# Loading the first shift vector ahead of the first weights of a decoder trunk

## The chip, the cores and the metric

The kernel runs on one core of a Trainium2 chip: TensorE for matmuls, VectorE, ScalarE and GpSimd for elementwise work, and SyncE (SP), which issues the transfers from HBM. They run beside each other and are ordered by semaphores alone; each does its own instructions in program order. The metric is the device time of one execution in microseconds. Before the change it is 1204.11 us, the median of 3 runs (1202.5 to 1204.75).

## The reference

Two layers, each with a half-step SwiGLU FFN, a token-mixing sub-layer and a second half-step FFN, all modulated by vectors that are computed from c; batch 1, 256 positions, 1024 channels, FFN width 2816.

```python
def modulate(x, g, shift, scale):
    return rmsnorm(x, g) * (1 + scale[:, None, :]) + shift[:, None, :]

c_act = jax.nn.silu(c)
for l in range(DEPTH):
    mod = c_act @ w_ada[l] + b_ada[l]
    sh1, sc1, gt1, sh2, sc2, gt2, sh3, sc3, gt3 = jnp.split(mod, N_MOD, axis=-1)
    h = modulate(x, ln_ffn1_g[l], sh1, sc1)
    x = x + 0.5 * gt1[:, None, :] * swiglu(h, ffn1_w_gate[l], ffn1_w_up[l], ffn1_w_down[l])
    ...
```

Each modulation vector is the product of c_act (1024) with a 1024x1024 part of w_ada, 4 MB of HBM. The change concerns the first two of the program: sc1 and sh1 of layer 0.

## The kernel before

All weights stream through four buffers of 1 MB (`raw`), in granules of one megabyte, in a fixed list (`seq`, filled by `adaunit` and `plan_ffn`). SP issues the transfer of a granule when the one four places ahead of it in the list has been used up. A weight granule holds two units of 128x1024. Each unit is split: ScalarE casts it to a high part (`hi`), and VectorE, or GpSimd for the units that `cfg["lo_first"]` names at the start, subtracts to get the low part (`lo`). There are six buffers for pairs of hi and lo. An FFN block of 128 columns then is 24 matmuls of 128x128 by 128x256: hi weights by hi input, hi by lo, lo by hi, eight each.

A modulation vector comes in four granules. VectorE multiplies each half granule with a column of c_act and adds it to a running sum of 128x1024 (`Lb` or `adaacc`, eight operations in `ada_step`); TensorE turns the sum, and VectorE reduces it to a column per block of 128 channels (`extract`, `complete`).

The list begins with the scale vector sc1 (`adaunit(0, 1, i)`), then come the granules gate 0, up 0 and gate 1 of the first FFN, then the shift vector sh1, then up 1 and so on. FFN blocks run in pairs q: two gate and two up units per q, and the two down units of the pair before.

The shift vector is late, so the first FFN begins without it. `G` holds x scaled by sc1 in high and low parts, not yet divided by the norm of each position (`S6a`, `Q`, `S3a`, `V`, `v`). `first()` runs six raw units on it with `low_last` (gate 0 and 1, up 0 and 1, gate 2 and 3). When the sum of sh1 is there, it multiplies the two-column shift with the same six units' weights (96 small products, `sh_b`) for their biases, and makes the true input H (`modulate`, high part on ScalarE, low part on VectorE; the product `PT` of scaled x and rstd on ScalarE and GpSimd). The raw outputs are multiplied by rstd afterwards (`normed_out`) and get the bias in `first_act`. `columns(0, 1)` transposes constants of the layer (`rowsA`, `rowsB`) into the one PSUM bank `x`, one after the other: the second transpose needs VectorE's copy of the first (`colA`). `keep_warm` issues three products that nobody reads.

The order of instructions on each engine is the order in which this program emits them. `pump` and `done` emit the next conversions of weights whenever a buffer of the six is free by a built-in model of the clock (`Clock`). All instructions are recorded in one helper line, L171; the tiles' names tell them apart.

In later phases sh and sc are known early: the shift then rides along as two more columns of the raw input (258 in place of 256), and four units run block by block in `first_units`.

## Time and profile before

| | |
|---|---|
| median of 3 runs | 1204.11 us |
| profiled execution | 1202.57 us, of which the span shown is 1200.8 us |
| TensorE busy | 1130.7 us (94% of the span) |
| VectorE busy | 874.4 us (73%) |
| ScalarE busy | 612.6 us (51%) |
| GpSimd busy | 169.3 us (14%) |
| mean granted TensorE clock | 0.976 of full speed |

The share of busy time of an engine says little by itself: what counts is which engine the others wait for in a stretch. The profile gives the chain of waits, followed back from the last instruction, and the timeline of each engine with the idle time ahead of an instruction and who ended it. The granted clock is 1.00 at 2.4 GHz and 0.50 at 1.2 GHz.

### The profile page before, as it was taken

The numbers are of one execution on the slowest core, as the hardware profiler recorded it, in microseconds if no ns is written. First come the engines' busy times: TensorE is split into PE (matmuls) and PEld (weight loads), VectorE is DVE, ScalarE is ACT, GpSimd is POOL, SyncE is SP. The second block draws the span as 40 slices with busy tenths as digits, with TensorE's granted clock in tenths as the row PEclk, the third lists the DMA queues.
The fourth block names the chain that finished last, engine by engine and source line by source line (L and its number), as shares of the span: only waits on it lengthen the run. The fifth ranks groups of instructions, "written<-read, shape, count | busy, mean of one in ns | idle before, by whom it ended". The sixth has DMA issues, their size and how long they took to land.

```text
span 1200.8 us, 22053 instructions
## 1 busy us (share of the span) xinstructions
PE 1130.7 (94%) x9085; PEld 1052.0 (88%) x9085; DVE 874.4 (73%) x1314; ACT 612.6 (51%) x1049; POOL 169.3 (14%) x213
## 2 busy tenths in 40 slices
PE   5799999999978789999999999999997899999997
PEld 4799999977767789999999999997876789999996
DVE  5778878757965788877778878774886759866554
ACT  4364443548367464434456544444654667544443
POOL 0610000011761010000000000001067401000001
PEclk9899999999999989999999999999999799999999
DMA  8759888836342558969865987892642334876640
GB/s 320 246 186 319 309 299 309 256 113 192 95 137 91 176 176 285 322 243 326 291 218 170 324 313 266 278 300 74 186 140 73 141 108 140 287 257 211 195 139 36
DMA packets 167661, 256.52 MB, mean 214 GB/s; under 512 B 8272, under 2 KB 134056, under 8 KB 167560
## 3 DMA queue, kind: packets, MB, share of 16 engines
q1 hardware_dynamic: 166536, 252.95, 62.6%
q0 software_dynamic: 1024, 2.16, 0.9%
q8 instruction: 71, 1.16, 0.4%
q14 instruction: 30, 0.25, 0.1%
HBM read 252.86 MB, written 2.23 MB: 212 GB/s over the span
## 4 chain that ended last, share of the span: by engine, by line
PE 71%; DVE 12%; ACT 6%; POOL 6%; issue 3%; DMA 1%; SPq 0%; POOLq 0%; DVEq 0%; ACTq 0%
PE pm L171 45%; PE pa L171 25%; DVE lo L171 3%; DVE adaacc L171 3%; PE px L171 2%; ACT hi L171 1%; POOL W L171 1%; POOL cacc L171 1%; POOL T L171 1%; POOL Lb L171 1%; DVE mod L171 1%; ACT L171 1%; DVE tmp L171 1%; DVE Lb L171 1%; DVE Y L171 1%
## 5 line engine op out<-in xcount | busy, mean ns | idle before, releaser
L171 PE MATMUL pm<-H,hi 128*128 128x256 f32 x2816 | 507.7, 283 | 2.8 <-issue 1.6
L171 DVE TENSOR_TENSOR lo<-raw,hi 128x1024 fp32r<-128x1024 f32 (+1 forms) x300 | 362.1, 1226 | 131.8 <-ACT hi L171 131.3
L171 PEld LDWEIGHTS pm<-H,hi 128*128 128x128 f32 x2816 | 431.9, 189 | 5.9 <-issue 2.2
L171 ACT CAST hi<-raw 128x1024 fp32r<-128x1024 f32 (+1 forms) x306 | 311.3, 1040 | 195.3 <-PE pm L171 80.7
L171 PE MATMUL pm<-H,lo 128*128 128x256 f32 x1408 | 392.4, 280 | 1.2 <-DVE lo L171 1.2
L171 PEld LDWEIGHTS pm<-H,lo 128*128 128x128 f32 x1408 | 264.5, 189 | 1.7 <-DVE lo L171 1.6
L171 PE MATMUL pa<-Y,hi 128*128 128x256 f32 x1312 | 241.3, 286 | 4.5 <-DVE xT L171 4.5
L171 PEld LDWEIGHTS pa<-Y,hi 128*128 128x128 f32 x1312 | 204.1, 192 | 6.7 <-DVE xT L171 5.3
L171 PE MATMUL pa<-Y,lo 128*128 128x256 f32 x656 | 185.8, 283 | 0.0
L171 PEld LDWEIGHTS pa<-Y,lo 128*128 128x128 f32 x656 | 127.3, 194 | 0.0
L171 POOL TENSOR_TENSOR xin_LT<-xin_LT 128x256 f32<-128x256 f32 x35 | 27.1, 775 | 664.8 <-ACT xin_LT L171 662.4
L171 ACT CAST Y<-tmp 128x256 fp32r<-128x256 f32 x88 | 35.8, 406 | 131.5 <-DVE tmp L171 131.5
L171 DVE SCALAR_TENSOR_TENSOR adaacc<-raw,c_act,adaacc 128x1024 f32<-128x1024 f32 x70 | 95.5, 1365 | 1.6
L171 DVE SCALAR_TENSOR_TENSOR Lb<-raw,c_act,Lb 128x1024 f32<-128x1024 f32 x56 | 71.8, 1283 | 4.2 <-DMA raw<-in_w_ada_dram 3.0
L171 POOL TENSOR_TENSOR cacc<-cacc,ctap 128x256 f32<-128x256 f32 x54 | 52.3, 973 | 122.0 <-DVE cacc L171 112.8
L171 DVE TENSOR_TENSOR Y<-tmp,Y 128x256 fp32r<-128x256 f32 x88 | 37.4, 425 | 41.5 <-ACT Y L171 41.5
L171 PE MATMUL pm<-Y,raw 128*128 128x256 f32 x288 | 66.8, 384 | 0.0
L171 PEld LDWEIGHTS pm<-Y,raw 128*128 128x128 f32 x288 | 53.4, 190 | 8.9 <-issue 1.0
L171 PE MATMUL pa<-hi,Y 128*128 128x512 f32 x176 | 54.8, 393 | 0.0
L171 ACT ACTIVATE tmp<-pm 128x256 f32<-128x256 f32 x84 | 31.8, 378 | 43.9 <-PE pm L171 43.7
L171 DVE TENSOR_REDUCE mod<-px 128x4 f32<-128x512 f32 x34 | 23.4, 689 | 34.3 <-PE px L171 34.2
L171 DVE SCALAR_TENSOR_TENSOR cacc<-hc,colB,cacc 128x256 f32<-128x256 f32 x66 | 36.0, 562 | 10.3 <-POOL cacc L171 9.4
(309 smaller groups left out, 1342.9 us busy)
## 6 DMA issues: line engine op xcount, KB each, us to landing
raw<-in_w_ada_dram SPq DMA_DIRECT2D x70, 1024.0 KB
raw<-in_ffn_w_gate_dram SPq DMA_DIRECT2D x44, 1024.0 KB
raw<-in_ffn_w_up_dram SPq DMA_DIRECT2D x44, 1024.0 KB
raw<-in_ffn_w_down_dram SPq DMA_DIRECT2D x44, 1024.0 KB
raw<-in_w_in_dram SPq DMA_DIRECT2D x12, 1024.0 KB
raw<-in_w_in_dram SPq DMA_DIRECT2D x20, 512.0 KB
raw<-in_w_out_dram SPq DMA_DIRECT2D x16, 512.0 KB
raw<-in_w_in_dram SPq DMA_DIRECT2D x4, 768.0 KB
```

The lines of the kernel that those rows point to most:

```text
L171: return getattr(real, op)(*args, **kw)
```

## The change

The granules of sh1 come right behind those of sc1, ahead of all weights. Its sum is shared: of each granule VectorE adds one half into `adaacc`, and TensorE multiplies the other half with a column of c_act into a row of 1x512 in each of two PSUM banks (`ada_rows`); at the end TensorE adds VectorE's sum to the rows with a product with ones, VectorE copies the row out, and eight transposes turn it into columns. The shift is then known ahead of the first unit, so `first()` is the one of the later phases: four units on 258 columns, one unit behind the other (`first_serial`, with `low_last`). The bias products, the raw units of gate 2 and 3 and `keep_warm` are gone. The other modulation vectors in the first FFN start at slot 2 in place of slot 4.

```diff
@@ -309,7 +309,7 @@
-        start = 4 if key == ("f", 0, 1) else 0
+        start = 2 if key == ("f", 0, 1) else 0
@@ -323,9 +323,6 @@
-                if key == ("f", 0, 1) and (q, n) == (1, "g"):
-                    for i in range(4):
-                        adaunit(0, 0, i)
@@ -406,8 +403,9 @@
-    for i in range(4):
-        adaunit(0, 1, i)
+    for v in (1, 0):
+        for i in range(4):
+            adaunit(0, v, i)
@@ -477,9 +475,39 @@
+    def ada_rows(raw, g, i):
+
+        if i == 0:
+            ada_acc[0, 0] = [ps([1, 512], f"a{2 + h}") for h in range(2)] + [sb([128, D], "adaacc")]
+        *rows, acc = ada_acc[0, 0]
+        halves = [slice(512 * h, 512 * h + 512) for h in range(2)]
+        for h in range(2):
+            mm(rows[h], c_act[:, 2 * i + 1:2 * i + 2], raw[:, 1, halves[h]], i == 0, False)
+        c = c_act[:, 2 * i:2 * i + 1]
+        if i == 0:
+            dve.tensor_scalar(acc, raw[:, 0], c, 0.0, op0=OP.mult, op1=OP.add)
+        else:
+            dve.scalar_tensor_tensor(acc, raw[:, 0], c, acc, op0=OP.mult, op1=OP.add)
+        release(g)
+        if i < 3:
+            return
+        row = sb([1, D], "Lb")
+        for h in range(2):
+            mm(rows[h], ones[:, 0:1], acc[:, halves[h]], False)
+            dve.tensor_copy(row[:, halves[h]], rows[h])
+        p = ps([128, KB], "x")
+        for k in range(KB):
+            pe.transpose(p[:, k:k + 1], row[:, 128 * k:128 * k + 128], ident[0:1, 0:1])
+        m = sb([128, KB], "mod0", bufs=2)
+        dve.tensor_copy(m, p)
+        complete(m, 0, 0, slice(0, KB))
+        mods[0, 0] = m
+
...
@@ -773,6 +803,11 @@
+    def first_serial(keys, outs, G, between):
+
+        for i, (key, o) in enumerate(zip(keys, outs)):
+            low_last(o, need(key), G["parts"], between if i == 0 else None)
+
...
@@ -897,93 +928,36 @@
...
-                keep_warm(3)
-                for h in range(2):
-                    extract()
...
-                for h in range(2):
-                    for i, kk in enumerate(keys):
-                        for k in range(4 * h, 4 * h + 4):
-                            for x, w in enumerate(conv[kk]):
-                                mm(p[i // 4][:, i % 4], both[:, k], w[:, k], k == 0 and x == 0 and i % 4 == 0, (k, x) == (KB - 1, 1))
...
+            opening = key == ("f", 0, 1)
+            (first_serial if opening else first_units)(keys, outs, G, lambda: norm.update(h=normed([pump] * 3, opening)))
+            for i in range(2):
+                for j in range(2):
+                    dve.tensor_copy(cols[i][:, j:j + 1], outs[2 * j + i][:, S:S + 1])
+            su = [normed_out(o) for o in outs]
+            acc.extend(ps([128, 2, S], f"a{i}") for i in range(4))
+            for kk in keys:
+                done(kk)
+            if opening:
                 columns(0, 1)
...
+            act.preload_act_table_set("silu_and_others")
+            for i in range(2):
+                first_act(i, su[i], su[2 + i], cols[i][:, 0:1], cols[i][:, 1:2])
+            return norm["h"]
...
@@ -1921,18 +1895,24 @@
-    cfg["lo_first"] = ["gp", "dve", "gp", "dve", "gp", "gp", "dve", "gp", "dve", "gp"]
     columns(0, 0)
-    step_stream()
     gs = need_mod(0, 1)
     G = begin(gs, None)
-    keep_warm(3)
+    rstd(sums)
     for k in range(KB):
         scaled_hi(G, k)
-        scaled_lo(G, k)
-    step_stream()
-    rstd(sums)
-    for _ in range(4):
+    for i in range(4):
+        step_stream()
+        for k in {1: range(4), 2: range(4, KB)}.get(i, ()):
+            scaled_lo(G, k)
+    cfg["lo_first"] = ["gp", "gp"]
+    G["sh"] = mods[0, 0]
+    for _ in range(2):
+        step_stream()
+    G["shift"](G["sh"])
+    for k in range(KB):
+        dve.scalar_tensor_tensor(nscr["t"][:, k], xT[:, k], gs[:, k:k + 1], nscr["r"], op0=OP.mult, op1=OP.mult)
+    for _ in range(2):
         step_stream()
```

Where the instructions stand now. On VectorE, from the last operation on the scale vector (mod_181 in before) to the first transposed constants, in before:

```order
L171 SCALAR_TENSOR_TENSOR mod_181<-mod_181,colA 128x4
L171 SCALAR_TENSOR_TENSOR S3a<-xT,mod_181,S6a 128x256 x3
L171 SCALAR_TENSOR_TENSOR V<-xT,mod_181,S6a 128x256 x3
L171 SCALAR_TENSOR_TENSOR v<-xT,mod_181,Q_199 128x256 x2
L171 TENSOR_TENSOR lo<-raw,hi 128x1024 x2
L171 TENSOR_SCALAR adaacc<-raw,c_act 128x1024
L171 SCALAR_TENSOR_TENSOR adaacc<-raw,c_act,adaacc 128x1024 x7
L171 COPY colA<-px 128x23
L171 COPY colB<-px 128x98
```

The same place now, from the same operation (mod_174 is the scale vector) to the shift vector, mod_253:

```order
L171 SCALAR_TENSOR_TENSOR mod_174<-mod_174,colA 128x4
L171 TENSOR_SCALAR adaacc<-raw,c_act 128x1024
L171 SCALAR_TENSOR_TENSOR adaacc<-raw,c_act,adaacc 128x1024
L171 SCALAR_TENSOR_TENSOR S3a<-xT,mod_174,S6a 128x256 x3
L171 SCALAR_TENSOR_TENSOR V<-xT,mod_174,S6a 128x256
L171 SCALAR_TENSOR_TENSOR adaacc<-raw,c_act,adaacc 128x1024
L171 SCALAR_TENSOR_TENSOR V<-xT,mod_174,S6a 128x256 x2
L171 SCALAR_TENSOR_TENSOR v<-xT,mod_174,Q_192 128x256 x2
L171 SCALAR_TENSOR_TENSOR adaacc<-raw,c_act,adaacc 128x1024
L171 COPY Lb<-pa_206 1x512
L171 COPY Lb<-pa_207 1x512
L171 COPY mod_253<-px 128x8
```

The sum of the shift (adaacc) has moved ahead of the weights' low parts and in between the low parts of the raw input, and has four operations in place of eight.

On VectorE behind the raw units in before (H_562 is the low part of H, tmp the raw outputs times rstd, bias_631 the row of bias products):

```order
L171 TENSOR_TENSOR lo<-raw,hi 128x1024
L171 SCALAR_TENSOR_TENSOR H_562<-PT,mod_445,H_561 128x256
L171 TENSOR_TENSOR tmp_591<-pa_246,rstd 128x256
L171 TENSOR_TENSOR tmp_593<-pa_247,rstd 128x256
L171 TENSOR_TENSOR tmp_595<-pa_246,rstd 128x256
L171 TENSOR_TENSOR tmp_597<-pa_247,rstd 128x256
L171 TENSOR_TENSOR lo<-raw,hi 128x1024
L171 TENSOR_REDUCE bias_631<-pa_624 128x6
```

The same place now, behind the four units (pm_296, pm_297, pa_298 and pa_299 are their outputs):

```order
L171 COPY bias_294<-pm_296 128x1
L171 COPY bias_294<-pa_298 128x1
L171 COPY bias_295<-pm_297 128x1
L171 COPY bias_295<-pa_299 128x1
L171 TENSOR_TENSOR tmp_422<-pm_296,rstd 128x256
L171 TENSOR_TENSOR tmp_424<-pm_297,rstd 128x256
L171 TENSOR_TENSOR tmp_426<-pa_298,rstd 128x256
L171 TENSOR_TENSOR tmp_428<-pa_299,rstd 128x256
L171 TENSOR_TENSOR lo<-raw,hi 128x1024 x4
L171 COPY colA<-px 128x23
L171 COPY colB<-px 128x98
```

The copies of the transposed constants (colA, colB) stand behind four low parts of weights now; in before they stood behind the sum of the shift.

On TensorE at the end of the raw units in before (rowsA and rowsB are the constants that are transposed, pm_249 the sixth unit):

```order
L171 MATMUL pm_249<-S6a,lo 128x256 x6
L171 MATMUL pm_249<-Q_199,lo 128x256 x2
L171 MATMUL px<-kc,rowsA 128x23
L171 MATMUL px<-kc,rowsB 128x98
L171 MATMUL pa_441<-xin_LT,ones 128x256 x3
L171 MATMUL px<-kc,adaacc 128x128 x4
L171 MATMUL pa_455<-kc,adaacc 128x128 x4
L171 MATMUL pa_433<-hi,sh_b 2x128
```

The same place now, at the end of the fourth unit (pa_299):

```order
L171 MATMUL pa_299<-S6a,lo 128x258 x6
L171 MATMUL pa_299<-Q_192,lo 128x258 x2
L171 MATMUL px<-kc,rowsA 128x23
L171 MATMUL px<-kc,rowsB 128x98
L171 MATMUL pm_467<-H_316,hi 128x256
```

The two transposes of constants stand at the same place behind the units, but what is queued behind them is the matmuls on H, where it was the turning of the shift's sum.

## Rows read from the trace of the kernel before

**Rows 1.** Busy time by stretches of the first FFN: from and to in us, length, then busy us and (instructions) of TensorE, its weight loads, VectorE, ScalarE and GpSimd; granted clock, share of the DMA engines, GB/s.

```profile
76.00:100.00 24.00, 24.00 (x206) 24.00 (x205) 19.35 (x22) 11.91 (x17) 0.00 (x0) 1.00 0.80 279
100.00:125.00 25.00, 25.00 (x216) 25.00 (x215) 19.17 (x22) 12.13 (x18) 0.00 (x0) 1.00 0.93 331
...
200.00:225.00 25.00, 25.00 (x214) 25.00 (x213) 21.59 (x23) 10.47 (x14) 0.00 (x0) 1.00 0.95 315
```

**Rows 2.** The chain of waits of the first 110 us: start, length, what.

```profile
33.62 2.82 DVE adaacc L171
...
48.16 1.63 DVE adaacc L171
...
61.52 2.62 DVE H L171
...
70.51 5.65 PE pa L171 x48
76.17 11.31 PE pm L171 x96
```

**Rows 3.** Timeline of TensorE: start, length, operation, out<-in, shapes, count, and in brackets the idle ahead and who ended it. A float product of 256 columns on ones is recorded as two.

```profile
22.73 0.60 PE L171 MATMUL pa<-kc,Lb 128*128 128x128 f32 x4
24.68 1.56 PE L171 MATMUL pa<-xin_LT,ones 128*128 128x256 f32 x6 [1.34 <-DVE mod L171]
25.89 1.11 PE L171 MATMUL pa<-S6a,hi 128*128 128x256 f32 x6
...
43.89 0.23 PE L171 MATMUL px<-kc,rowsA 23*128 23x23 f32 x1
49.93 0.42 PE L171 MATMUL px<-kc,rowsB 98*128 98x98 f32 x1 [5.81 <-DVE colA L171]
50.15 2.82 PE L171 MATMUL pa<-xin_LT,ones 128*128 128x256 f32 x6
...
64.18 0.38 PE L171 MATMUL pm<-H,hi 128*128 128x256 f32 x1 [1.22 <-DVE H L171]
64.50 0.53 PE L171 MATMUL pa<-kc,Wc 2*128 2x2 f32 x6
...
66.46 3.11 PE L171 MATMUL pm<-H,hi 128*128 128x256 f32 x16
69.41 1.10 PE L171 MATMUL pm<-H,lo 128*128 128x256 f32 x8
...
76.00 0.40 PE L171 MATMUL pm<-H,hi 128*128 128x256 f32 x2
```

**Rows 4.** Timeline of VectorE.

```profile
6.70 0.75 DVE L171 TENSOR_SCALAR Lb<-raw,c_act 128x1024 f32<-128x1024 f32 x1 [3.77 <-DMA raw<-in_w_ada_dram]
7.49 1.28 DVE L171 SCALAR_TENSOR_TENSOR Lb<-raw,c_act,Lb 128x1024 f32<-128x1024 f32 x1
...
23.94 0.68 DVE L171 TENSOR_REDUCE mod<-pa 128x4 f32<-128x512 f32 x1
...
24.93 1.27 DVE L171 SCALAR_TENSOR_TENSOR S3a<-xT,mod,S6a 128x256 fp32r<-128x256 f32 x3
...
36.47 13.32 DVE L171 SCALAR_TENSOR_TENSOR adaacc<-raw,c_act,adaacc 128x1024 f32<-128x1024 f32 x7
...
61.52 2.61 DVE L171 SCALAR_TENSOR_TENSOR H<-PT,mod,H 128x256 fp32r<-128x256 f32 x1
```

**Rows 5.** Timelines of ScalarE, GpSimd and SP's queue (a DMA row there is the issue of a transfer).

```profile
27.27 1.03 ACT L171 CAST hi<-raw 128x1024 fp32r<-128x1024 f32 x1
54.78 0.20 ACT L171 CAST sh_b<-mod 128x4 fp32r<-128x4 f32 x1 [18.68 <-DVE mod L171]
...
38.65 12.40 POOL L171 TENSOR_TENSOR PT<-PT,rstd 128x256 f32<-128x256 f32 x8
61.37 2.47 POOL L171 TENSOR_TENSOR lo<-raw,hi 128x1024 fp32r<-128x1024 f32 x1 [10.32 <-ACT hi L171]
...
68.85 0.37 SPq L171 DMA_DIRECT2D raw<-in_ffn_w_gate_dram  x1
```

**Rows 6.** Half microseconds: length, TensorE busy (instructions), granted clock, share of the DMA engines, GB/s. Here the last two columns are read.

```profile
28.00:28.50 0.50, 0.50 (x7) 1.00 0.33 115
...
73.50:74.00 0.50, 0.50 (x6) 1.00 0.07 21
```

**Rows 7.** The same view; here the granted clock is read.

```profile
48.00:48.50 0.50, 0.00 (x0) 0.85 0.95 371
...
55.00:55.50 0.50, 0.27 (x5) 0.82 0.03 8
...
65.00:65.50 0.50, 0.50 (x5) 0.92 0.19 16
...
68.50:69.00 0.50, 0.50 (x5) 0.67 0.00 0
```

**Rows 8.** Timeline of VectorE in the first units of the second FFN phase (layer 0, second FFN), where the shift rides along as two more columns.

```profile
447.57 0.15 DVE L171 COPY bias<-pm 128x1 f32<-128x1 f32 x1
...
447.84 0.74 DVE L171 TENSOR_TENSOR tmp<-pm,rstd 128x256 f32<-128x256 f32 x2
...
449.16 2.35 DVE L171 TENSOR_TENSOR lo<-raw,hi 128x1024 fp32r<-128x1024 f32 x2
451.43 0.74 DVE L171 TENSOR_SCALAR Lb<-raw,c_act 128x1024 f32<-128x1024 f32 x1
```

More of the change, by code (lines that the diff above doesn't have):

```diff
@@ L673, in begin, with shift @@
         los = [pieces[2][:, k] for k in range(3)] + [pieces[3][:, k] for k in range(3)] + [pieces[4][:, k] for k in range(2)]
-        if sh is not None:
+        def shift(sh):
             hi, lo = split_col(sh)
@@ L677, in begin @@
                 dve.tensor_copy(pieces[piece][:, :, S:S1], src[:, k:k + n].unsqueeze(2).to_broadcast([128, n, S1 - S]))
-        return dict(gs=gs, sh=sh, parts=[(a[:, :S1 if sh is not None else S], b[:, :S1 if sh is not None else S])
-                                         for a, b in zip(his, los)])
+        if sh is not None:
+            shift(sh)
+        return dict(gs=gs, sh=sh, parts=list(zip(his, los)), shift=shift)
     def begin_whole(gs, sh, w):
@@ L960, in first @@
-            if G["sh"] is not None:
-                su = [normed_out(o) for o in outs]
-                acc.extend(ps([128, 2, S], f"a{i}") for i in range(4))
-                for kk in keys:
-                    done(kk)
-                act.preload_act_table_set("silu_and_others")
-                for i in range(2):
-                    first_act(i, su[i], su[2 + i], cols[i][:, 0:1], cols[i][:, 1:2])
-                return norm["h"], None
-            return norm["h"], turn_row
-        bias, raws = [], []
@@ L972, in ffn @@
-        hparts, pending = first()
+            cols = [sb([128, 2], f"bias{i}") for i in range(2)]
+            outs = [bank((128, S1)) for _ in range(2)] + [ps([128, S1], f"a{i}") for i in range(2)]
+            norm = {}
+            opening = key == ("f", 0, 1)
[3 more added lines that the diff above has]
+                    dve.tensor_copy(cols[i][:, j:j + 1], outs[2 * j + i][:, S:S + 1])
@@ L976, in ffn @@
         for q in range(1, FB // 2):
[L977 to L978 removed]
+            o = [bank() for _ in range(2)]
+            blocks = [(j, i, key + (n, 2 * q + i)) for j, n in enumerate("gu") for i in range(2)]
             for j, i, kk in blocks:
                 w = need(kk)
[L981 to L986 removed]
+                for k in range(KB):
+                    mm3(o[i][:, j], w, hparts, lambda a: a[:, k], lambda a: a[:, k], k == 0, k == KB - 1)
                 done(kk)
```

67 lines of the change are left out of this document (6 added, 61 removed).

## The prediction

> **What bounds the kernel now.** I read four views, in this order: busy time by stretches, the chain of waits of the first 110 us, the timelines of the engines up to 76 us, and the granted clock in half microseconds. From 76 to 225 us, which is nearly the whole first FFN, TensorE is busy without a gap and VectorE for 77 to 86% [rows 1]: the first FFN is bound by TensorE, and what the change does to the end is read from one point, the start of the third pair of gate and up blocks (q=2). In before it is at 76.00 us [rows 3]. Behind it each engine keeps nearly the order it had, and behind the first FFN it is the same, so the end should move as that point moves.
>
> Ahead of it the chain goes through VectorE's sum of the first shift vector (33.6 to 49.8 us), the turning of that sum on TensorE, and the low part of H, to the down products at 70.51 [rows 2]. TensorE does six raw units (144 matmuls) from 25.89 to 43.89 us, waits 5.81 us, and does the bias products, two up units and two down units until 76.00 [rows 3]. The granted clock fell from 2.4 to 1.2 GHz at 48.35 us, rose at 55.18, fell at 65.42 and rose at 68.83: a mean of 0.85 in a half microsecond is 0.35 us at 1.00 and 0.15 at 0.50, and so on [rows 7].
>
> **The change, part by part.** I follow TensorE to the same q=2 block. Until 25.0 us nothing is different: VectorE's last small operation on the scale vector ends there, when S3a starts [rows 4].
>
> 1. The shift's granules. Nine megabytes (x, four scale and four shift granules) must land ahead of the first weights. In before nine also landed first (three of them weights), and the transfers died down at 28.0 to 28.5 us [rows 6]. So the last shift granule is there by 28.3 at the latest, and nobody wants it before 31.7. This costs the chain nothing.
>
> 2. VectorE's half of the sum. From 25.0: a TENSOR_SCALAR 0.75, to 25.75; one SCALAR_TENSOR_TENSOR 1.28, to 27.0; four low parts of the raw input at 0.42 (three take 1.27), to 28.7; 1.28, to 30.0; four more, to 31.7; the last sum, to 33.0 [rows 4]. In before eight such operations went on to 49.8.
>
> 3. TensorE's half, eight products of one column with 512 float columns. The trace has none. The nearest row is the product with ones on 256 columns: three in 1.21 us at the full clock (24.68 to 25.89) and three in 2.61 at the half (50.15 to 52.76) [rows 3], so 0.81 or 1.74 us for 512. They begin at 23.3 us, behind the turning of the scale vector [rows 3]. At 0.81 all are done by 30.3, with a short wait for the bank that VectorE's reduction empties at 24.6 [rows 4]: hidden behind VectorE until 33.0. At 1.74 they would not be. I take 0.81, since TensorE ran at that rate at 24.68, and keep the other as a rival.
>
> 4. From the sums to the first unit, all of it open: two products with ones, the first at 0.81 and the second at 1.74 because TensorE has by then idled since 30.3; a copy of 512 elements from PSUM (0.69 as for the reduction of 512 [rows 4]); the last four transposes, about 0.35 (six small ones took 0.53 [rows 3]); then six dependent small steps through VectorE and ScalarE at 0.16 to 0.20 (the one on ScalarE is 0.20 [rows 5]), with hand-overs some 1.2. That is 33.05 + 0.81 + 1.74 + 0.69 + 0.35 + 1.2 = 37.85 us.
>
> 5. GpSimd beside it. The first gate granule can be asked for when the first shift granule is used up, at 25.8. A weight granule asked for at 68.85 brought its last bytes just after 73.5 [rows 5, 6], 4.8 us later, so this one is there at 30.6, ScalarE's cast takes 1.0 [rows 5], and GpSimd starts the first of two low parts at about 31.65. VectorE's last sum wants to start at 31.7. In before a low part of H asked for at 61.52, just behind GpSimd's start at 61.37, took 2.61 us in place of 0.42, and ended 0.3 us behind GpSimd's 2.47 [rows 4, 5]. So the last sum is late by nothing or by 2.4 us (if VectorE goes first, GpSimd is in the way of the small steps instead, for about 1). I take 1.2, the middle, since the two starts lie within the error of my sum: the first unit starts at 39.0.
> A milder row: beside GpSimd's eight PT products of 256 elements, seven sums took 13.32 us [rows 4, 5], 1.90 each with the long first one. The Trainium skill, page "SBUF — State Buffer", section "Terms", says that the two engines share one port pair as an exclusive lock held for the whole instruction, so that the loser stands still. By that rule the long GpSimd operation costs a whole instruction (37.85 + 2.4 = 40.25), by the seven sums some 0.6 (38.45); the row of H bears the rule out.
>
> 6. Four units in a row: 96 matmuls. 48 took 5.65 us and 96 took 11.31 in the chain [rows 2], 0.118 each: 11.3, so 50.3. Their own inputs are early: GpSimd's two low parts are done before 38, and VectorE makes the next ones while TensorE is at work on the first two units.
>
> 7. A new stop. In program order VectorE now does the last bias copy, four products with rstd, four low parts of weights, and only then the copy of the first transposed constants (colA); TensorE can't begin the second transpose, into the same bank, before that copy, and all H matmuls are queued behind the transpose. In the second FFN phase this part of VectorE's work is seen: four copies from 447.57 to 447.84, four products to 449.16, two low parts to 451.43, 1.14 each [rows 8]. So 0.15 (last matmul) + 0.07 + 1.32 + 4.54 + 0.22 + 0.22 (second transpose, 49.93 to 50.15 [rows 3]) = 6.5 us of an idle TensorE. In before the same copy also came late, but there TensorE had to wait for the shift's sum anyway.
>
> 8. Then 96 matmuls on H (two gate, two up units) and 48 of the down products: 144 × 0.118 = 17.0. The 96 bias products, the two turnings of the shift vector and keep_warm are gone; they are inside the 76.00 of before.
>
> 9. The clock. TensorE now stops twice, from 30.3 to 39.0 with little in between, and for 6.5 us. In before the clock fell after an idle of 4.2 us, and again after 1.2 us of idle with only small work about it. It rose 5.25 us after TensorE resumed at 49.93, and the second stretch at 1.2 GHz lasted 3.4 us [rows 3, 7]. In it sixteen matmuls took 2.95 us (66.46 to 69.41), 0.58 of them at the full clock: ten in about 2.3, 0.22 each against 0.118 [rows 3]. So a microsecond at half clock loses 0.47 us, one stop 1.6 to 2.5, the two 3.2 to 5.0; nothing if the clock holds. I take 4.0.
>
> Sum: 39.0 + 11.3 + 6.5 + 17.0 + 4.0 = 77.8 us against 76.0: 1.8 us later. The profiled execution took 1202.6 (a span of 1200.8 and 1.8 around it) and would become 1204.4. The median of the runs is 1.5 us above it, and on it the prediction is 1205.9. The terms' bounds (port 0 to 2.4, clock 3.2 to 5.0) make 75.8 to 80.2, so 1203.9 to 1208.3.
>
> **Rivals.**
> Faster: the clock holds. If the row products and the products with ones keep TensorE at 2.4 GHz through the first stop, the second stop doesn't lower it, and GpSimd comes after the last sum, 37.85 - 0.9 (the second product with ones at 0.81) + 11.3 + 6.5 + 17.0 = 71.75, which is 4.2 us earlier: 1199.9. For it: 1.3 us of idle from 23.3 to 24.68 did not lower the clock. Against it: 1.2 us did at 64, and the second stop is longer than the idle that lowered it at 48.35 [rows 3, 7].
>
> Slower: the row products set the start. It decides from 1.2 us for each of the eight on; at the half-clock price of 1.74 they end at 23.3 + 13.9 = 37.2, the products with ones follow in 3.5, and with 0.69, 0.35 and 1.2 the first unit starts at 42.9, 3.9 later than forecast: 81.7, 1209.8. For it: a product with a single column appears in no row. Against it: while TensorE did the 96 two-column bias products of before, the granted clock stayed at 1.00 [rows 7].
>
> No change, because the shift was never in the way: the chain of before has its sum on it for 16 us, but the six raw units would end at 43.89 in any case. If the stop of part 7 were short (the four low parts done ahead), the block would start 4.5 us earlier, at 73.3: 1201.4. In program order nothing allows it, and I give it little.
>
> Something in the rest of the first FFN: the other shift and scale granules now begin two slots earlier, which puts VectorE's sums among the low parts sooner. VectorE has some 20% to spare there [rows 1]; some 2 us to either side.
>
> **How the numbers follow.** Forecast 0.68, clock holds 0.10, row products 0.10, stop short 0.05, rest of the FFN 0.07. What a measurement of this kernel can tell from no change is about 0.2%, 2.4 us: faster is below 1201.7, slower above 1206.5. The forecast alone gives 0.40 within and 0.28 above. Clock holds and stop short give 0.11 faster and 0.04 within; the row products 0.10 slower; the rest 0.02 faster, 0.03 within, 0.02 slower. Together 0.13, 0.47, 0.40. The range takes the forecast's own bounds, a part of the faster cases below and the nearer half of the row products above: 1201.6 to 1209.3.
>
> **What would show it.** In the profile of after: the first matmul of 258 columns at 37.9 to 40.3 us; VectorE's last sum at about 33 us, or 35.4 if it took 2.5 or more beside GpSimd; row products of about 0.8 us, done by 30.5. An idle of about 6 us ahead of the second transpose of constants, released by VectorE's colA, with four low parts just ahead of the copy. Two stretches of 0.50 in the granted clock, of 3 to 5 us, at the start of the first unit and of the H matmuls. And the third pair of blocks at 75.8 to 80.2. I am wrong if TensorE has no stop behind the fourth unit, if the clock stays at 1.00, or if TensorE has gaps between there and 225 us.

## The result and the profile after

The changed kernel takes 1214.26 us (median of 4 runs, 1212.83 to 1216.13), the kernel before beside it 1203.86 (4 runs): a ratio of 1.0099, with a 95% interval of 1.0079 to 1.0119. It is slower by 10.4 us, where 1.8 was forecast, and lies above the range.

| | before | after |
|---|---|---|
| profiled execution | 1202.57 us, span 1200.8 | 1214.54 us, span 1212.8 |
| TensorE busy | 1130.7 us | 1139.7 us |
| mean granted TensorE clock | 0.976 | 0.968 |

The opening first, since the prediction is about it. TensorE's timeline of after, with the idle ahead of a row and its releaser in brackets (a float product of 512 columns is recorded as two):

```profile
23.52 4.45 PE L171 MATMUL pa<-raw,c_act 128*1 128x512 f32 x10 [0.39 <-DVE mod L171]
28.47 1.88 PE L171 MATMUL pa<-raw,c_act 128*1 128x512 f32 x4 [0.50 <-DMA raw<-in_w_ada_dram]
31.46 1.88 PE L171 MATMUL pa<-adaacc,ones 128*1 128x512 f32 x4 [1.11 <-DVE adaacc L171]
...
37.56 1.63 PE L171 MATMUL pm<-S6a,hi 128*128 128x258 f32 x6 [3.05 <-DVE S3a L171]
...
51.86 0.24 PE L171 MATMUL px<-kc,rowsA 23*128 23x23 f32 x1
58.13 0.42 PE L171 MATMUL px<-kc,rowsB 98*128 98x98 f32 x1 [6.04 <-DVE colA L171]
...
77.85 0.40 PE L171 MATMUL pm<-H,hi 128*128 128x256 f32 x2
```

And VectorE's and GpSimd's:

```profile
30.13 1.28 DVE L171 SCALAR_TENSOR_TENSOR adaacc<-raw,c_act,adaacc 128x1024 f32<-128x1024 f32 x1
...
35.29 2.05 DVE L171 TENSOR_TENSOR sh_l<-mod,sh_h 128x8 fp32r<-128x8 f32 x1 [0.26 <-ACT sh_h L171]
...
53.36 4.62 DVE L171 TENSOR_TENSOR lo<-raw,hi 128x1024 fp32r<-128x1024 f32 x4
57.90 0.17 DVE L171 COPY colA<-px 128x23 f32<-128x23 f32 x1
...
32.65 4.66 POOL L171 TENSOR_TENSOR lo<-raw,hi 128x1024 fp32r<-128x1024 f32 x2 [32.19 <-ACT hi L171]
```

Compare [rows 3, 4]. VectorE's last sum is done at 31.4, the first unit of 258 columns starts at 37.56, the four units end at 51.9, the second transpose of constants waits 6.04 us behind four low parts and the copy of colA, and the third pair of blocks (q=2) starts at 77.85, against 76.00 in before. This point moves with the execution: in seven profiles with the opening of before (before, the control, runs 2, 6, 7, 14 and 16 below) it lies at 74.20 to 76.00, mean 75.25, and in four with the changed opening (after, runs 1, 15 and 17) at 76.26 to 78.21, mean 77.5. So the opening costs some 2.2 us, and a single pair of profiles tells it only to a microsecond or two. The two stretches at half clock:

```profile
36.00:44.00 8.00, 6.43 (x32) 6.47 (x33) 8.00 (x18) 7.03 (x13) 1.31 (x1) 0.57 0.77 267
56.00:64.00 8.00, 5.87 (x28) 5.88 (x29) 5.27 (x9) 2.57 (x5) 0.00 (x0) 0.57 0.72 258
```

In half microseconds the granted clock is 0.96 at 36.0 and 0.71 at 43.0, 0.94 at 56.5 and 0.73 at 63.5. So it fell at 36.46 and 56.94 and rose at 43.29 and 63.77: 6.83 us at 1.2 GHz each time, of which 5.73 and 5.64 lie behind the point where TensorE resumes (37.56 and 58.13). The rest of the first FFN reads like [rows 1]: TensorE without a gap, at the full clock, VectorE with time to spare.

```profile
76.00:100.00 24.00, 24.00 (x206) 24.00 (x205) 19.96 (x20) 10.05 (x13) 0.00 (x0) 1.00 0.91 306
100.00:125.00 25.00, 25.00 (x213) 25.00 (x212) 19.06 (x24) 10.72 (x15) 0.00 (x0) 1.00 0.91 326
200.00:225.00 25.00, 25.00 (x214) 25.00 (x213) 19.80 (x20) 10.63 (x13) 0.00 (x0) 1.00 0.98 327
```

So far no time is lost beyond the forecast. The rest is lost later. The table has the start of VectorE's last operation on xT in each phase of both profiles; TensorE's and VectorE's instructions between stand in the same order in both.

| end of | before | after | later by |
|---|---|---|---|
| layer 0, first FFN | 238.72 | 240.72 | 2.0 |
| layer 0, mixing | 435.58 | 442.01 | 6.4 |
| layer 0, second FFN | 631.09 | 637.68 | 6.6 |
| layer 1, first FFN | 820.55 | 828.86 | 8.3 |
| layer 1, mixing | 1006.45 | 1015.59 | 9.1 |
| the span | 1200.8 | 1212.8 | 12.0 |

Ten of the twelve microseconds arise where the change altered no instruction: 4.4 and 0.8 in the two mixing phases, and 0.2, 1.7 and 2.9 in three FFNs that TensorE fills. These are one profile each: the control below, the kernel before once more, has 236.41, 434.27, 630.49, 819.95, 1006.31 and 1200.7, by which 7.8 of 12.1 us arise there, so a phase's share is known to some 2 us. The loss needs two causes. In these FFNs TensorE is busy for 99% of the time, and yet it is slower: these rows are its H products in the last FFN (from, to, length, busy time and count, granted clock, share of DMA, GB/s), first of before, then of after.

```profile
1016.50:1182.00 165.50, 114.43 (x960) 1.00 0.60 198
```

```profile
1025.50:1194.00 168.50, 116.74 (x960) 1.00 0.59 194
```

The same 960 products at the same clock take 2.31 us more; in the two FFNs between they take 116.81 and 116.90 us against 115.88 and 115.98. In the mixing it is a stop. First before, then after, TensorE's timeline around the small 32 x 32 products:

```profile
363.40 1.01 PE L171 MATMUL pa<-Wc,Lb 32*32 32x32 f32 x95
364.67 0.84 PE L171 MATMUL pa<-kc,E 128*128 128x128 f32 x3 [0.25 <-ACT E L171]
...
949.40 0.77 PE L171 MATMUL pm<-H,hi 128*128 128x256 f32 x2 [1.57 <-issue]
```

```profile
364.87 0.86 PE L171 MATMUL pa<-Wc,Lb 32*32 32x32 f32 x78
368.82 0.44 PE L171 MATMUL pa<-Wc,Lb 32*32 32x32 f32 x17 [3.09 <-issue]
...
953.74 0.75 PE L171 MATMUL pa<-Wc,Lb 32*32 32x32 f32 x63
957.63 0.65 PE L171 MATMUL pa<-Wc,Lb 32*32 32x32 f32 x32 [3.14 <-issue]
```

In after TensorE stops in the middle of one run of 95 equal products, behind the 78th in layer 0 and behind the 63rd in layer 1, for 3.1 us each, and the profile knows no releaser ("issue"). In before the first such run goes through, and the one stop of the kind (1.57 us) is at 949.40. The experiments are about these two causes.

### The profile page after: what moved, and what is told of

Its sections match the earlier page's. It is cut to its first block, busy times and chain, and to the rows that moved or that the text cites. A ratio compares the mean times of both kernels' runs of the same rounds, so it can differ in the third digit from the quotient of the medians.

```text
span 1212.8 us, 21867 instructions
## 1 busy us (share of the span) xinstructions
PE 1139.7 (94%) x8991; PEld 1055.0 (87%) x8991; DVE 868.1 (72%) x1327; ACT 609.4 (50%) x1038; POOL 144.7 (12%) x201
## 3 DMA queue, kind: packets, MB, share of 16 engines
q8 instruction: 70, 1.15, 0.4%
## 4 chain that ended last, share of the span: by engine, by line
PE 74%; DVE 11%; POOL 6%; ACT 4%; issue 3%; DMA 1%; SPq 0%; POOLq 0%; ACTq 0%; DVEq 0%
PE pm L171 46%; PE pa L171 27%; DVE lo L171 3%; PE px L171 2%; DVE adaacc L171 2%; POOL W L171 1%; ACT hi L171 1%; POOL cacc L171 1%; POOL T L171 1%; POOL Lb L171 1%; DVE Lb L171 1%; DVE tmp L171 1%; DVE mod L171 1%; ACT L171 1%; DMA xin_LT<-in_x_dram 1%
## 5 line engine op out<-in xcount | busy, mean ns | idle before, releaser
L171 PE MATMUL pm<-H,hi 128*128 128x256 f32 x2848 | 522.9, 286 | 0.0
L171 DVE TENSOR_TENSOR lo<-raw,hi 128x1024 fp32r<-128x1024 f32 (+1 forms) x304 | 366.2, 1221 | 149.8 <-ACT hi L171 149.7
L171 PEld LDWEIGHTS pm<-H,hi 128*128 128x128 f32 x2848 | 443.1, 191 | 2.6 <-issue 0.3
L171 PE MATMUL pm<-H,lo 128*128 128x256 f32 x1424 | 404.0, 284 | 1.3 <-DVE lo L171 1.3
L171 PEld LDWEIGHTS pm<-H,lo 128*128 128x128 f32 x1424 | 270.8, 190 | 1.7 <-DVE lo L171 1.7
L171 PEld LDWEIGHTS pa<-Y,lo 128*128 128x128 f32 x656 | 124.3, 189 | 0.0
L171 DVE SCALAR_TENSOR_TENSOR adaacc<-raw,c_act,adaacc 128x1024 f32<-128x1024 f32 x66 | 86.2, 1307 | 1.4
```

The lines of the kernel that those rows point to most:

```text
L171: return getattr(real, op)(*args, **kw)
```

## The experiments

Medians stand against the kernel before on the same chip: 1201.36 us in runs 1 to 4, 1201.48 in 5 to 8, 1201.39 in 9 to 12, 1202.65 in 13 to 15 and the control, 1201.84 in 16 and 17.

### Where the tiles lie: runs 1, 2, 5, 6 and 7

A tile's SBUF address follows from the order in which names are first asked for, and the change asks in another order. So H moved from 181824 to 178816, the ring Y from 164288 to 168512, and the weights' tiles too. Runs 1 and 2 exchange the addresses alone, by asking for all names ahead of everything, in the other kernel's order:

```diff
+LAYOUT = (("kc", 1), ("gr", 1), ("xin_LT", 1), ("eps", 1), ("F", 2),
...
+    for tag, n in LAYOUT:
+        for _ in range(n):
+            pool.tile([128, 16 if tag == "sh_b" else 8], F32, name=tag, tag=tag, bufs=n)
```

Run 1 (the changed kernel, old addresses):

> The changed kernel with every tile at the SBUF address that it has in the kernel before; order and instructions are untouched. In the changed kernel the tiles of the weights (hi, lo) and of H stand at other addresses, because their names are first asked for in another order. Addresses theory: the blocks of 96 H matmuls take 11.31 us again in place of 11.39 to 11.6 and the down blocks 5.45 to 5.65 in place of 5.66 to 5.74, so that the kernel comes down from about 1214 to 1208 to 1210. Rival (addresses are nothing, the slower blocks come from the rotation of the PSUM banks or from the instants at which things meet): it stays at 1213 to 1216 with blocks of 11.39. Rival (it is all the opening and the clock in the mixing): 1213 to 1216.

Run 2 (the kernel before, new addresses):

> The kernel before with every tile at the SBUF address that it has in the changed kernel; order and instructions untouched. Addresses theory: the H blocks take 11.39 to 11.5 in place of 11.31 behind the first FFN and the kernel goes from about 1204 to 1208 to 1210. Rivals: 1203 to 1205 with blocks of 11.31.

Measured: run 1 1207.36 us (ratio 1.0048, 1.0030 to 1.0067), run 2 1207.65 (1.0055, 1.0039 to 1.0071). Each kernel has the other's pace in the last FFN, to the hundredth; run 1, then run 2:

```profile
1019.00:1185.00 166.00, 114.43 (x960) 1.00 0.60 197
```

```profile
1017.00:1187.00 170.00, 116.74 (x960) 1.00 0.58 192
```

So the addresses are worth 6.3 us on the kernel before (run 2), and with the old addresses the change's ratio goes from 1.0099 to 1.0048. That is half of the loss. Which tile it is, runs 6 and 7 ask, by lists of names that bring H alone, or the weights and Y alone, to their addresses of after (first the line of run 6, then that of run 7, against the list of before).

```diff
-    ("sh_b", 1), ("mod0", 2), ("Wc", 1), ("H0", 1), ("H1", 1),
+    ("sh_b", 1), ("mod0", 2), ("bias0", 1), ("bias1", 1), ("H0", 1), ("H1", 1),
...
-    ("colB", 2), ("hi", 6), ("lo", 6), ("mod1", 2), ("S6a", 1),
+    ("colB", 2), ("mod1", 2), ("S6a", 1), ("Q3", 1), ("S3a", 1), ("V", 1), ("v", 1),
+    ("adaacc", 1), ("mod0", 2), ("hi", 6), ("lo", 6), ("sh_h", 1), ("sh_l", 1), ("Y", 1),
+    ("vb", 1), ("H0", 1), ("H1", 1), ("tmp2", 4),
```

> The kernel before with H alone at the addresses of the changed kernel (178816 and 187008 in place of 181824 and 190016), the weights' tiles where they were. If H's address decides, blocks of 11.39 and more and 1207 to 1208 where before has 1201 to 1204, as in the run with all addresses; if the weights' tiles decide, 11.31 and no change.

> The kernel before with the tiles hi and lo of the weights (and with them Y and the small tiles between) at the addresses of the changed kernel, H where it was. The other half: blocks of 11.39 and more and 1207 to 1208 if the weights' tiles decide, 11.31 and no change if H does. If both runs show a part, it is the two together or the tiles' distance.

Run 6 takes 1203.12 us (1.0017, 1.0005 to 1.0029), run 7 1203.48 (1.0012, 0.9994 to 1.0030). The H products, first of run 6, then of run 7:

```profile
1012.00:1182.00 170.00, 117.12 (x960) 1.00 0.59 192
```

```profile
1016.00:1182.00 166.00, 114.22 (x960) 1.00 0.60 197
```

H's own address sets the pace of the products that read H (117.12 us); moving the weights' tiles doesn't change it here (114.22), and they lie at a multiple of 256 bytes in both kernels (96512 and 119296). The down products in run 7, which read Y (moved from 192 to 64 modulo 256), took 63.3 us in the last FFN against 62.25 in before. The two halves add to 3.6 us of time, where run 2 has 6.3; the intervals nearly cover the difference, and whether there is more is open.

Run 5 takes everything else away: it leaves out the whole computation and has nothing but products on zeros, with H and the weights at chosen addresses.

```diff
+    def unit(name, h, w, hl=8192, wl=24576, n=2):
...
+            for k in range(KB):
+                for x, y in ((0, 0), (0, 1), (1, 0)):
+                    nc.tensor.matmul(o, at(w + x * wl + 512 * k, 128), at(h + y * hl + 1024 * k, 256),
+                                     start=r == 0 and k == 0 and (x, y) == (0, 0), stop=True, skip_group_check=True)
```

> A kernel of matmuls alone (all data zero, the output is not the reference's): units of 24 or 48 products of 128 x 128 weights with 256 float32r columns, in the order of an H block, at chosen SBUF addresses and with no other engine at work. First the addresses of the kernel before and of the changed one for H and for the weights, and both crossed; then H, the weights, the distance of the low weights and of the low part of H in steps of 64 bytes. Static addresses theory: the pairs of before run at 113.3 to 117.8 ns a product, those of the changed kernel at 118.5 to 122, and one of the series shows a step. Rival (the address matters only against the writes of other engines and of the DMA): all units run at one rate within 0.5 ns.

```profile
72.58 11.55 PE L201 MATMUL newH_newW<-every 128*128 128x256 f32 x96
83.96 11.47 PE L201 MATMUL oldH_newW<-every 128*128 128x256 f32 x96
95.27 11.55 PE L201 MATMUL newH_oldW<-every 128*128 128x256 f32 x96
106.66 11.47 PE L201 MATMUL oldH_oldW<-every 128*128 128x256 f32 x96
...
152.06 5.86 PE L201 MATMUL Ha<-every 128*128 128x256 f32 x48
157.75 5.82 PE L201 MATMUL Hb<-every 128*128 128x256 f32 x48
163.41 5.91 PE L201 MATMUL Hc<-every 128*128 128x256 f32 x48
169.16 5.82 PE L201 MATMUL Hd<-every 128*128 128x256 f32 x48
174.81 5.86 PE L201 MATMUL He<-every 128*128 128x256 f32 x48
180.51 5.63 PE L201 MATMUL Hf<-every 128*128 128x256 f32 x48
185.98 5.90 PE L201 MATMUL Hg<-every 128*128 128x256 f32 x48
```

Read the starts: 96 products take 11.39 us with H where after has it (72.58 to 83.96, 95.27 to 106.66), 11.31 where before has it, whichever weights go with it. With no other engine at work these are the block times that the expectations name for the two kernels. Ha to Hf are 48 products each, H at 128, 192, 0, 64, 128 and 192 modulo 256 bytes. From start to start the 48 take 5.69, 5.66, 5.75, 5.65, 5.70 and 5.47 us, and the ten units that follow repeat the last four figures. At 192 a product so takes 114.0 ns in three units of four and 117.8 in the other, 117.8 at 64 (before), 118.6 at 128 (after), 119.7 at 0. The series on the weights moved by 64 bytes shows steps of the same size (118.6, 117.8, 120.0, 117.8 at 0, 64, 128 and 192).

### The opening: runs 4 and 8

Run 4 puts the two transposes of constants, and their copies, ahead of the four low parts; run 8 does so at the old addresses.

```diff
+            if opening:
+                columns(0, 1)
             for kk in keys:
                 done(kk)
-            if opening:
-                columns(0, 1)
```

> The changed kernel with the two transposes of constants and their copies ahead of the four low parts of weights, so that TensorE doesn't wait for them. Theory of the prediction (the stop of 6 us stands on the chain): TensorE waits for the first low part instead, some 2.5 us, and the third pair of blocks starts 3 to 5 us earlier than 77.8 (5 if the second half-clock stretch shortens too), and the end comes earlier by the same: 1209 to 1211. If the rest of the program takes what it gets by its own clock and not by the shift, the end moves by another amount than that point, up to 5 us either way.

> The changed kernel with both: every tile at its address of before, and the two transposes of constants ahead of the four low parts. If the two costs add, 1207.4 (constants earlier, new addresses) less the 5.5 to 6.4 that the addresses were worth in the two runs with all addresses exchanged: some 1201, no slower than the kernel before. If the time saved in the first FFN is given back in the mixing by the clock, 1204 to 1206.

Run 4: 1207.42 us (1.0047, 1.0033 to 1.0061), where the changed kernel stands at 1.0099: some 6 us less, more than the 3 to 5 expected. Run 8: 1198.87 (0.9980, 0.9968 to 0.9993), which is 2.6 us faster than the kernel before. The stop of part 7 was on the chain: without it the first FFN ends at 231.86 in run 8, where run 1, the same but for the constants, has 237.07. That is 6.9 us earlier than in before, and the two mixing phases give back 2.8 and 2.2 of it.

### The mixing: runs 3, 9, 10, 11 and the control

Runs 3, 9 and 10 are the kernel before with seven, four and ten products ahead of the third pair of blocks, which nobody uses; in run 11 the seven stand behind the raw units, in TensorE's idle time at 43.9 us. First the edit of runs 3, 9 and 10, then that of run 11.

```diff
         for q in range(1, FB // 2):
+            if key == ("f", 0, 1) and q == 2:
+                p = ps([128, S], "x")
+                for _ in range(7):
+                    nc.tensor.matmul(p, ones, nscr["r"], start=True, stop=True, skip_group_check=True)
...
                     low_last(o, need(kk), G["parts"])
+                w = ps([128, S], "x")
+                for _ in range(7):
+                    nc.tensor.matmul(w, ones, nscr["r"], start=True, stop=True, skip_group_check=True)
```

> The kernel before with seven products with ones on 256 columns (their result is not used) on TensorE ahead of the third pair of gate and up blocks: at 0.40 us each the rest is 2.8 us late, and nothing else is touched. My prediction's step (behind that point the end moves as the point moves): 1204 + 2.8 = 1206.6, with the half-clock stretches of both mixing phases as before (two of 10.2 us in the second, none between 349 and 410 us). Clock theory (a shift of the instants is enough for TensorE to lose its clock once more in the mixing): a third stretch at half clock as in the changed kernel, and 1209 to 1213.

> The kernel before with four products with ones (not used by anything) ahead of the third pair of blocks, in place of the seven that cost 6.0 where 2.4 to 2.8 were given. It gives 1.4 to 1.6 us. Theory of instants (whether TensorE loses its clock in the mixing hangs on when its idle stretches fall): the excess over the delay isn't in proportion to it, and somewhere between one and ten products it is near zero or below. Theory of a longer TensorE stream or of any delay at all: 1.5 and the same 3 to 4 us of excess, 1206.

> The same with ten products, 3.6 to 4.0 us. Theory of instants: another excess than with four and seven, 1201.4 + 3.8 = 1205 if there is none. Theory of any delay: 3.8 and 3 to 4 of excess, 1208 to 1209.

> The kernel before with the seven unused products in the 5.8 us in which TensorE waits for the first shift vector (from 43.9 us), so that they delay nothing and may even keep the clock up for a while. If a longer TensorE stream makes the excess, 1205 to 1206 with no delay in the first FFN; if the delay or the instants do, 1200 to 1203.

> The kernel before unchanged, for another profile of it. If the half-clock stretch at 364 to 375 us belongs to the other kernels (all of the delayed and changed ones showed it), this profile has none there and the time is 1200 to 1203; if it belongs to the execution, it may show it, and then the profile of before that the prediction read was a lucky one in the mixing.

| run | products | ratio | over before | given | stops on "issue" in the profile |
|---|---|---|---|---|---|
| 9 | 4 | 1.0048 (1.0032 to 1.0065) | 5.1 us | 1.6 | 0.69 + 2.54 |
| 3 | 7 | 1.0052 (1.0033 to 1.0071) | 6.2 us | 2.8 | 1.24 + 5.29 |
| 10 | 10 | 1.0085 (1.0066 to 1.0103) | 9.2 us | 4.0 | 2.88 + 2.77 |
| 11 | 7, in idle time | 1.0013 (1.0000 to 1.0027) | 1.8 us | 0 | 1.96 + 2.98 |
| control | none | 1202.50 us | | | 1.77 |

My theory of instants fell: the excess is there at every delay and has no zero. The other one named, that a longer TensorE stream makes it, comes nearer: by the stops it is the place in the stream that counts, and not its length (after has 8991 products, before 9085). All six profiles with the TensorE stream of before (before, the control, runs 2, 6, 7 and 14) have one stop of 1.56 to 1.83 us and no other of 0.3 us or more; every other stream has other stops, or none. The stops don't give each row's excess to the microsecond: they are from one profile each, and in run 11 the two stops would make 3.4 us more than before has, and 1.8 was measured. But they are tied to a count, not to an instant. TensorE's products from the start of the span to the stop, in after (both stops), in before, and in run 10:

```profile
0.00:368.80 368.80, 332.79 (x2511) 0.97 0.69 231
0.00:957.60 957.60, 894.31 (x7098) 0.97 0.67 225
```

```profile
0.00:949.30 949.30, 889.77 (x7227) 0.98 0.68 227
```

```profile
0.00:371.20 371.20, 335.12 (x2640) 0.97 0.67 229
0.00:956.85 956.85, 894.86 (x7227) 0.97 0.66 225
```

The count is 7227 in before, in the control and in runs 3, 9, 10 and 11, and 2639 or 2640 for their first stop; it is 2511 and 7098 in after and in runs 1, 8, 12 and 15. Whatever product comes next waits. In before 2622 products are done when the run of 95 is through (at 364.60), so the 2640th comes behind it, among wider products, and no stop is recorded there. Ten products more ahead, each recorded as two, put the boundary inside the run, behind its 93rd:

```profile
367.39 0.99 PE L171 MATMUL pa<-Wc,Lb 32*32 32x32 f32 x93
371.26 0.31 PE L171 MATMUL pa<-Wc,Lb 32*32 32x32 f32 x2 [2.88 <-issue]
```

The profile also hints at what is waited for. The page has a queue that carries instructions, and around the first stop of after (366.3 to 367.5 us) one transfer of it, while none is there from 343.0 to 366.3:

```profile
q8 instruction: 70, 1.15, 0.4%
```

```profile
q8 instruction: 1, 0.02, 5.1%
```

70 transfers in 1.15 MB are 16 KB each. TensorE's last product ahead of the stop ends at 365.73, the block comes between 366.3 and 367.5, and products go on at 368.82. Runs 1 and 10 have the same order at their first stops: one block between 362.4 and 363.5 us and products again at 364.74, one between 368.9 and 370.0 and products again at 371.26. That TensorE waits for this block is read from these times; the profile names no releaser.

A rival is the clock, which was lower in after: 0.83 over 341 to 391 us, against 0.97 in before. The profiles on hand settle it for the first mixing phase. These rows are that whole phase (length, TensorE's busy time, then the granted clock), of before, of run 6, which has no stop there, and of after:

```profile
238.72:435.58 196.86, 173.93 (x1370) 0.95 0.46 145
```

```profile
237.02:433.48 196.46, 180.66 (x1382) 0.90 0.44 146
```

```profile
240.72:442.01 201.29, 177.54 (x1382) 0.92 0.44 141
```

Run 6 has a lower clock than after and takes no longer than before. All seven profiles without a stop of 0.3 us in this phase (before, the control, runs 2, 6, 7, 13 and 14) take 195.9 to 197.9 us at clocks of 0.90 to 0.95; the twelve with a stop of 0.7 to 3.7 us take 198.3 to 202.3. There the stop makes the loss, not the clock. In the second mixing phase no pair of profiles separates the two.

### What the stops are worth: runs 12 to 17

Run 12 is run 8 with H 128 bytes further on, at 192 modulo 256; runs 14 and 15 are before and the changed kernel at these addresses.

```diff
-    ("mod0", 2), ("Wc", 1), ("H0", 1), ("H1", 1), ("tmp2", 4),
+    ("mod0", 2), ("Wc", 1), ("gap", 1), ("H0", 1), ("H1", 1), ("tmp2", 4),
...
-            pool.tile([128, 16 if tag == "sh_b" else 8], F32, name=tag, tag=tag, bufs=n)
+            pool.tile([128, 32 if tag == "gap" else 16 if tag == "sh_b" else 8], F32, name=tag, tag=tag, bufs=n)
```

> The best version so far (constants earlier, addresses of before: 1198.9) with H 128 bytes further on, at 192 in place of 64 modulo 256 (181952 and 190144). In the kernel of products alone this place ran at 114.0 ns a product in three of four units and at 117.8 in the fourth, against 117.8 at 64. Theory that the address of the moving side sets the rate of the products: blocks of 96 at 10.95 to 11.31, and 3 to 15 us less, 1184 to 1196. Rival (other engines' traffic or the mixing decide): 1198 to 1200.

> The kernel before with H at 192 modulo 256 (181952 and 190144), all else as it was. If the rate of the products is the whole effect, 12 to 14 us less than before, as from the eighth to the twelfth run (1198.9 to 1186.0): 1187 to 1190. It is the base against which the change alone is to be judged at these addresses.

> The changed kernel as it is (constants behind the four low parts), with the addresses of before and H at 192. Against the fourteenth run it shows the opening alone, without addresses: by the prediction 1.8 us slower, by the run with old addresses (1207.4 against 1201.4) 5 to 6 slower, 1192 to 1196. If the mixing's clock then is the rest, the excess over the shift at the end of the first FFN is again in the two mixing phases.

Run 12: 1185.99 us (0.9877, 0.9857 to 0.9896); its H products in the last FFN:

```profile
1003.00:1168.00 165.00, 111.66 (x960) 1.00 0.60 198
```

Run 14: 1189.09 (0.9886, 0.9870 to 0.9902). Run 15: 1191.53 (0.9906, 0.9889 to 0.9924). At equal addresses the change alone costs 2.4 us here, near the 1.8 of the prediction, but the two intervals leave some 3 us to either side, and the two profiled executions are 5.1 us apart. Run 15's profile still has stops of 6.2 us against 1.75 in run 14, and its first FFN ends 0.5 earlier, so the nearness to 1.8 is luck.

Runs 13, 16 and 17 put eight unused products into each mixing phase, in run 12, in before and in run 1.

```diff
+        w = ps([128, S], "x")
+        for _ in range(8):
+            nc.tensor.matmul(w, ones, nscr["r"], start=True, stop=True, skip_group_check=True)
         tick_until("PT")
```

> The fastest version so far (1186.0) with eight unused products with ones on TensorE in each of the two mixing phases, at the place where it waits some 5 us for ScalarE's softmax (340.1 to 345.2 us in the kernel before); no other engine waits for them. If that wait is what takes the clock down in the mixing (half clock from 343.0 and from 366.9 us in the times of before), the stretch of 10.2 us goes and the second with it, and the time falls by 2 to 6 us. Rival: the clock falls later in the mixing all the same, over the shorter waits from 355 us on, or the products stand in the way of the chain: 1185 to 1188.

> The kernel before, with the eight unused products in the softmax gap of both mixing phases. Both profiles of before have no half-clock stretch between 364 and 375 us, so there is less to win than the 8 us of the thirteenth run: 2 to 5 us, 1197 to 1200.

> The changed kernel at the addresses of before (1207.4 in the first run, 5.2 to 5.8 more than before) with the same products in the gap. If the mixing's clock made the excess over the opening's own 1.8 to 2.4 us, the distance to the sixteenth run is now 1 to 3 us: 1199 to 1202, and it gains more by the products than before does. If the excess is something else, the distance stays at 5 to 6.

Run 13: 1177.88 us (0.9799, 0.9779 to 0.9819), the fastest of all, 8.1 less than run 12. Run 16: 1205.45 (1.0031, 1.0021 to 1.0042), 3.6 more than before where 2 to 5 less was expected. Run 17: 1202.65 (1.0009, 0.9998 to 1.0020). The products didn't land where I had put them: in run 13 they run at 341.6, behind the softmax gap. What they do change is the place of everything behind them in TensorE's stream. Run 13 has no stop of 0.3 us or more on "issue" at all, where run 12 has 3.64 and 3.41, and its run of 95 goes through:

```profile
350.76 0.92 PE L173 MATMUL pa<-Lb,Wc 32*32 32x32 f32 x69 [0.64 <-ACT E L173]
...
351.54 1.25 PE L173 MATMUL pa<-Wc,Lb 32*32 32x32 f32 x95
352.81 0.84 PE L173 MATMUL pa<-kc,E 128*128 128x128 f32 x3
```

Run 17 has one stop of 1.53 us, run 16 two (1.74 and 2.13). So the same eight products cost before 3.6 us and save the change 4.7 (by the ratios of runs 1 and 17), and with them the change at the old addresses is 2.8 us faster than before with them (against before as it is, it is the same within the interval). Products that only held up the clock would have gained in both kernels. So most of what was lost in the mixing isn't a property of the new opening, but of where the number of its instructions puts the boundaries.

## Why the prediction was wrong

The account of the opening holds in its mechanisms; in its sum errors cancel.

1. The shift's granules cost 0.50 us of waiting on TensorE (28.47) and nothing on the chain, as said.
2. VectorE's sum ended at 31.4, not 33.0: the opening ahead of it ran 1.2 us earlier than in before's profile. That isn't the edit alone: with the same instructions the scale vector is done at 25.12 us in run 1 and at 23.86 in after.
3. The row products ended at 30.35, against 30.3. That is luck in part, since they began 1.2 us early and took some 0.92 us each, not 0.81. The rival at 1.74 us each is out.
4. The two products with ones took 1.88 us together, not 2.55: the clock fell only at 36.46, behind them.
5. The gate granule took 6.9 us from its request (24.59) to the cast that waited for it (31.52), not 4.8. GpSimd began at 32.65 and hit the small step sh_l (2.05 us for 8 columns) in place of the last sum. That is the block that I had left as the second case, at nearly twice its price of 1. The first unit came at 37.56 against 39.0.
6. The four units took 14.3 us against 11.3 and the clock's share. At the full clock 24 products of 258 columns took 2.89 us, 0.120 each, so 0.3 is the products and some 2.6 the clock.
7. The stop is 6.04 us; with its neighbours it is 6.4 (51.9 to 58.3) against 6.5. The rival of a short stop is out.
8. and 9. From 58.3 to 77.85 it is 19.5 us against 17.0, 2.5 more of the clock. The clock so cost some 5.1 us against the 4.0 taken, just above the upper bound of 5.0: behind the two stops TensorE worked 5.73 and 5.64 us at half clock, where I had read 5.25 and 3.4 from before.

The start was 1.4 us early, the clock 1.1 dear and the products 0.3 dear, and q=2 came at 77.85 where 77.8 stood; with a spread of 2 us from execution to execution, so close a meeting is luck. (By the prediction's own terms the upper end of that point adds up to 80.0, not 80.2.) The clock didn't hold, and the rest of the first FFN added 0.15 us: none of the four rivals happened.

The step that failed is the sentence "Behind it each engine keeps nearly the order it had, and behind the first FFN it is the same, so the end should move as that point moves." The order is the same, and between the two profiles the point moved by 1.85 us and the end by 12.0. The sum put whatever follows that point at nothing, by the order alone. Two things that the order doesn't hold had changed with the edit: the addresses of tiles that it doesn't touch (about 6 us by runs 1 and 2), and the place of every later TensorE instruction in its stream (stops of 6.23 us in place of 1.57 in the two profiles, so 4.7). With the 2.0 of the first FFN these give 12.7 against the 12.0 of the spans. The terms come from different runs, so that agreement is known to no better than some 2 us. Run 15 against 14 and run 17 against 16 test the sentence again, with the addresses equal: 2.4 slower, and 2.8 faster, with stops of 6.2 against 1.75 us in the one pair and 1.53 against 3.87 in the other. The opening's own worth is therefore known to a few microseconds only.

Still open: why an address modulo 256 bytes sets the pace of a product, why only two block boundaries of some seventy stop TensorE for long, and how much of the time in the second mixing phase is the stop and how much the lower clock.

## What to carry to other kernels

When an edit adds, drops or reorders tiles, compare the built addresses of the operands that TensorE reads before reading its time: pin them (by asking for the names in a fixed order), and try H-like operands at the four places modulo 256; here that was worth 13 us (runs 8 and 12), more than the edit itself. Count the instructions of a stream too: a run of tiny products that meets such a boundary stopped here for some 3 us, and a few unused products ahead can move it away or into it, so a version is judged by its stops on "issue" as well as by its order. And what an opening gains or loses arrives at the end only if nothing between takes it: a table of the same instruction in each phase shows where it went, and a second profile of the unchanged kernel shows how much of it is the execution.

## What the runs showed that I had not expected

- The pace of a float32r product with 256 columns went with the address of its moving operand modulo 256 bytes: 114.0 to 119.7 ns in a kernel with no other work, 111.66 to 117.12 us for 960 of them in the last FFN, at a granted clock of 1.00.
- TensorE waited 0.7 to 5.3 us at fixed counts of products, 2511 and 7098 or 2640 and 7227, and the times of the 16 KB blocks on the instruction queue suggest that it waits for them. The Trainium skill, page "Runtime: NRT & Kernel Launch", section "Instruction fetch mechanics", says that instructions are refilled in blocks of 16 KiB, 256 instructions, and that the cost of crossing into the next is mostly hidden. The block size agrees with this trace (1.15 MB in 70). By that rule a crossing would cost next to nothing; if these stops are crossings, as their counts say, 3.09 and 3.14 us aren't hidden where products of 32 x 32 follow each other at some 10 ns. By that page a block would be 128 products with their weight loads, an estimate; the counts 2640 and 2511 are 129 apart, with the other instructions of the stream not counted. The queue has no engine's name, but 70 such blocks are 17920 instructions, by the same estimate, and TensorE's 8991 products and 8991 weight loads are 17982; before has 71 blocks (18176) and 18170 of them.
- An 8-column operation on VectorE took 2.05 us, from 35.29 to 37.34, beside GpSimd's two low parts, which ended at 37.31; the 8-column operation just before it took 0.27.
- The same opening differed by some 2 us from one execution to the next: q=2 at 74.20 to 76.00 us in before's, 76.26 to 78.21 in the changed one.
